# A hybrid encoder trunk on one NeuronCore: group A's softmax weights transposed as sixty-four-by-sixty-four quarters instead of whole 128 by 128 blocks

## The chip, the cores and the metric

The kernel runs on one NeuronCore of a Trainium2 chip. The metric is the device time of one execution in microseconds; the figure to compare is the median of several runs. The engines are named as in the profile: PE is TensorE's matmul, PEld its weight load, DVE VectorE, ACT ScalarE, POOL GpSimd, SP SyncE, which issues most DMAs.

## The reference

Two layers, each over 1024 tokens of 1024 channels. What matters here is group A, six heads of 64 channels whose attention runs over a mixture of three windows with dilations 1, 4 and 16:

```python
for (w, d) in DILATED_PAIRS:                      # (128,1), (512,4), (2048,16)
    half = w // (2 * d)
    ...
    o, l = banded_attention(to_sub(q), to_sub(k), to_sub(v), bias_table, half, half, d)
wts = jax.nn.softmax(jnp.stack(lses, 0), axis=0)
return jnp.einsum('gbsh,gbshd->bshd', wts, jnp.stack(outs, 0))
...
pexp = jnp.exp(logits - m[..., None])             # inside banded_attention
out = jnp.einsum('nbgrqk,nbkgd->nbqgrd', pexp, vb.astype(jnp.float32))
```

Beside group A a layer has windowed attention (group B), an mLSTM (group C), one input and one output projection, a SwiGLU feed-forward layer and a gated embedding.

## The kernel before, in words

Everything is float32. The large projections split each operand into a high and a low part and issue three matmuls per block of 128 rows (`product`, L219 to L221, 128x512 each); attention multiplies in plain float32.

`group_a` works on units `(p, g, i)`: three head pairs `p`, two groups of windows `g`, four steps `i`; 24 units in each layer, 48 in all. The heads of a pair are called `e` = 0, 1. A unit has three stages:

- `score` (L529 to L537): queries times keys for two tiles of 128 queries, each head into a PSUM bank of its own (`psc`). Bias and row maximum follow on DVE (L549), the exponential on ACT (L550); the result is `pr`, two tiles of 128 queries by 512 weights.
- `flip` (L555 to L570): each `pr` is turned so that keys stand on the partitions. Four 128 by 128 transposes on PE fill one bank (`ppt`, L563), one bank per head; DVE copies the first head's bank to SBUF (`pT`, L568), ACT the second's (L566).
- `weigh` (L572 to L597): `pT` times values into `po` (L584), copied to `u` on DVE (L587 to L592).

The steps are staggered: step `n` issues `score(n)`, `weigh(n-2)`, `flip(n-1)`. Between two steps PE works on the input projection. Which instruction of which stream comes next on PE is set by `mix`, which advances the streams by estimated costs (`yield` values); `flip` counts 1000 there, as before the change. The order inside DVE, ACT and POOL is chosen by the framework's scheduler when the program is built, from estimated durations, and is then fixed. PE has one queue for all streams: whatever stands behind a waiting matmul waits too.

While the first head pair is under way, a side stream computes the gates of group C (`gates`, L828 to L900): bias (L843, L844), exponentials on ACT (L845 to L849), then two pairs of scans on DVE (L858 `gb`, L859 `gm`), an exponential on ACT (L866 `q`) and short operations (L864 to L882). `combine_a` merges the windows; its matmuls with 64 columns of weights and 32 moving columns are L635. Group C's `weigh` has products with 64 columns of weights and 65 moving columns (L1007). The input projection's evacuations are L399 and L401 (`z`). PSUM has six rotating banks for all of these and two more for the projection.

Of the kernel before, what the change touches and what calls it, by code (L numbers as in the profile page):

```python
# [21 lines left out]
P = 128  # L22
# [60 lines left out]
class Trunk:  # L83
# [386 lines left out]
    def group_a(self, z):  # L470
# [3 lines left out]
        nc = self.nc  # L474
        units = [(p, g, i) for p in range(3) for g in range(2) for i in range(NCH // 2)]
        heads = (slice(0, 64), slice(64, 128))
# [78 lines left out]
        def flip(u):  # L555
            p, g, i = u
            pTs = []
            for e, pr in enumerate(st[u]):
                pt = self.bank("ppt")
                for b in range(4):  # L560

                    c = b if g == 0 else b % 2 * 2 + b // 2
                    nc.tensor.transpose(pt[:, c * P : c * P + P], pr[:, b * P : b * P + P], self.ident)  # L563
                pT = self.half("pT")
                if e:
                    nc.scalar.copy(pT, pt)  # L566
                else:
                    nc.vector.tensor_copy(pT, pt)  # L568
                pTs.append(pT)
            st[u] = pTs  # L570

# [26 lines left out]
        for i in range(n + 2):  # L598
            cost = 0.0
            if i < n:  # L600
                p = units[i][0]
                if units[i][1:] == (0, 0):
                    while ("k", p) not in z:
                        yield None
                    begin(p)
                    cost += 2000.0
                score(units[i])
                cost += 1000.0
                if units[i][1:] == (0, 3) and p < 2:
                    tables(p + 1)  # L610
            if 0 <= i - 2:
                weigh(units[i - 2])
                cost += 1000.0
            if 0 <= i - 1 < n:
                flip(units[i - 1])
                cost += 1000.0
            yield cost
# [1049 lines left out]
```

## Time and profile before

| what | value |
|---|---|
| median of 3 runs | 2799.74 us (2798.83 to 2800.63) |
| the profiled execution's own time | 2797.81 us |
| its span, first to last instruction | 2796.0 us |
| PE busy | 2670.7 us (96%), 13930 matmuls |
| DVE busy | 1920.4 us (69%) |
| ACT busy | 1129.1 us (40%) |
| mean granted TensorE clock | 0.978 of full speed |
| DMA, mean over the span | 92 GB/s |

The profiled execution took 1.8 us more than its span, and lies 1.9 us under the median. A row of the time line gives the start of an instruction or of a run of equal ones, how long it lasted, the engine, the line of the kernel, the operation, the tile written and those read, the shape and the count. For PE a shape such as 128*64 128x65 says how many rows and columns of the array were in use and what was streamed. Matmuls overlap, so what one of them costs is the distance between starts, not its duration. Of a matmul of plain float32 the trace shows more records than the program has instructions; counts in rows are of records.

### The profile page before, as it was taken

To read this page: it belongs to the slowest core of one execution; us is meant where nothing else is said; L and a number is where in the kernel's file an instruction comes from. 1 tells how busy PE (TensorE), PEld (TensorE's weight loads), DVE (VectorE), ACT (ScalarE), POOL (GpSimd) and SP (SyncE) were. 2 spreads that over 40 slices of the span, in tenths; PEclk is the share of its full clock that TensorE was granted. 3 is DMA by queue.
4 is the path that set the end of the run, shared out by engine and by line. 5 is a ranking of instruction groups with operands and counts; after the bars stand their busy time and mean duration, and the time that the engine had idled before them with its cause. 6 is when DMAs were issued, how large, how long until landed. Compare 5 with 4: busy or idle time off the path is not lost.

```text
span 2796.0 us, 37474 instructions
## 1 busy us (share of the span) xinstructions
PE 2670.7 (96%) x13930; PEld 2124.0 (76%) x13930; DVE 1920.4 (69%) x3019; ACT 1129.1 (40%) x2301; POOL 966.8 (35%) x724
## 2 busy tenths in 40 slices
PE   8999998998999999999999999989899999989997
PEld 6777776676888887788777778857678888877887
DVE  8654866579665558997655448564986565599957
ACT  5443253544333324344445433543443333333444
POOL 3112433136332325660121123431553333276302
PEclk9999999999999999999999999999899999999999
DMA  4010145132222235312321012542232222632124
GB/s 146 28 65 31 42 110 174 56 129 72 95 77 82 91 109 189 116 61 68 114 82 54 32 38 71 116 148 97 79 113 76 83 91 72 207 133 86 46 83 136
DMA packets 134618, 258.57 MB, mean 92 GB/s; under 512 B 14649, under 2 KB 55649, under 8 KB 134436
## 3 DMA queue, kind: packets, MB, share of 16 engines
q1 hardware_dynamic: 130740, 244.51, 26.7%
q0 software_dynamic: 3696, 11.66, 1.2%
q8 instruction: 110, 1.80, 0.3%
q14 instruction: 72, 0.59, 0.1%
HBM read 206.19 MB, written 49.93 MB: 92 GB/s over the span
## 4 chain that ended last, share of the span: by engine, by line
PE 77%; DVE 12%; issue 4%; POOL 2%; ACT 2%; DMA 2%; SPq 0%; DVEq 0%; POOLq 0%; ACTq 0%
PE pd L219 10%; PE pd L220 9%; PE pd L221 9%; PE pd L1270 9%; PE pd L1269 9%; PE pd L1271 9%; PE pd L1410 3%; PE pd L1411 3%; PE pd L1409 3%; PE po L584 1%; PE ppt L563 1%; DVE f L134 1%; DVE x L1234 1%; DVE x L1382 1%; DVE wr L1336 1%
## 5 line engine op out<-in xcount | busy, mean ns | idle before, releaser
L1270 PE MATMUL pd<-r,wf 128*128 128x512 f32 x1232 | 494.0, 401 | 16.4 <-POOL r L1229 9.3
L1269 PE MATMUL pd<-r,wf 128*128 128x512 f32 x1232 | 490.1, 398 | 11.3 <-ACT r L1228 11.3
L1271 PE MATMUL pd<-r,wf 128*128 128x512 f32 x1232 | 488.9, 397 | 0.0
L219 PE MATMUL pd<-h,wh 128*128 128x512 f32 x832 | 339.3, 408 | 12.7 <-ACT h L133 6.8
L220 PE MATMUL pd<-h,wh 128*128 128x512 f32 x832 | 329.4, 396 | 2.8 <-DVE h L134 1.7
L221 PE MATMUL pd<-h,wl 128*128 128x512 f32 x832 | 328.0, 394 | 1.0 <-DVE wl L134 1.0
L1288 DVE TENSOR_TENSOR g<-g,pd 128x512 f32<-128x512 f32 x264 | 176.8, 684 | 219.0 <-PE pd L1271 218.9
L1270 PEld LDWEIGHTS pd<-r,wf 128*128 128x128 f32 x1232 | 234.7, 191 | 81.7 <-POOL r L1229 19.2
L1269 PEld LDWEIGHTS pd<-r,wf 128*128 128x128 f32 x1232 | 235.1, 191 | 67.0 <-ACT r L1228 13.0
L1271 PEld LDWEIGHTS pd<-r,wf 128*128 128x128 f32 x1232 | 235.3, 191 | 52.3
L134 POOL TENSOR_TENSOR f<-wr,f 128x512 fp32r<-128x512 f32 x120 | 181.2, 1523 | 154.7 <-ACT f L133 127.9
L1410 PE MATMUL pd<-f,f 128*128 128x512 f32 x560 | 221.3, 395 | 12.9 <-DVE f L134 12.9
L1409 PE MATMUL pd<-f,f 128*128 128x512 f32 x560 | 220.3, 393 | 5.4 <-DVE x L1382 5.4
L1411 PE MATMUL pd<-f,f 128*128 128x512 f32 x560 | 220.8, 394 | 4.2 <-POOL f L134 4.1
L133 ACT CAST f<-wr 128x512 fp32r<-128x512 f32 x240 | 137.9, 619 | 192.6 <-PE pd L1410 90.7
L133 ACT CAST wf<-s 128x512 fp32r<-128x512 f32 x176 | 105.0, 619 | 272.4 <-POOL s L200 121.1
L134 DVE TENSOR_TENSOR wf<-s,wf 128x512 fp32r<-128x512 f32 x176 | 176.2, 1002 | 42.8 <-ACT wf L133 41.6
L134 POOL TENSOR_TENSOR wl<-wr,wh 128x1024 fp32r<-128x1024 f32 (+1 forms) x44 | 109.3, 2483 | 249.9 <-ACT wh L133 139.5
L219 PEld LDWEIGHTS pd<-h,wh 128*128 128x128 f32 x832 | 158.0, 190 | 48.1 <-ACT h L133 6.8
L220 PEld LDWEIGHTS pd<-h,wh 128*128 128x128 f32 x832 | 158.0, 190 | 35.2 <-DVE h L134 2.6
L221 PEld LDWEIGHTS pd<-h,wl 128*128 128x128 f32 x832 | 157.7, 189 | 35.5 <-DVE wl L134 1.9
L197 POOL TENSOR_TENSOR s<-wr,s 128x512 f32<-128x512 f32 x44 | 59.1, 1344 | 307.1 <-DVE wf L134 307.1
(315 smaller groups left out, 5484.2 us busy)
## 6 DMA issues: line engine op xcount, KB each, us to landing
wr<-w_up SPq DMA_DIRECT2D x88, 512.0 KB, 3.7
wr<-w_in SPq DMA_DIRECT2D x52, 512.0 KB, 3.6
gd<-g SPq DMA_DIRECT2D x88, 256.0 KB, 2.0
wr<-w_down SPq DMA_DIRECT2D x80, 256.0 KB, 4.2
wr<-gd SPq DMA_DIRECT2D x80, 256.0 KB, 5.3
wr<-ple_gate SPq DMA_DIRECT2D x40, 512.0 KB, 3.5
ee<-md SPq DMA_DIRECT2D x32, 384.0 KB, 7.5
x<-xd SPq DMA_DIRECT2D x24, 512.0 KB, 4.3
```

The costliest lines, as they stand in the source:

```text
L133: self.pin(nc.scalar.copy(hi[:, cs], src))
L134: self.pin((eng or nc.vector).tensor_tensor(lo[:, cs], src, hi.bitcast(F32)[:, cs], OP.subtract))
L219: nc.tensor.matmul(ps, hi[:, ks], rh, start=k == 0, stop=False)
L220: nc.tensor.matmul(ps, hi[:, ks], rl, start=False, stop=False)
L221: nc.tensor.matmul(ps, lo[:, ks], rh, start=False, stop=k == n - 1)
L1269: nc.tensor.matmul(ps, hi[:, ks], rh, start=k == 0, stop=False)
L1270: nc.tensor.matmul(ps, hi[:, ks], rl, start=False, stop=False)
L1271: nc.tensor.matmul(ps, lo[:, ks], rh, start=False, stop=k == KT // 2 - 1)
L1288: add = lambda out, a, b, op=OP.add: nc.vector.tensor_tensor(out, a, b, op)
L1409: nc.tensor.matmul(ps, lh[:, cs], rh, start=k == 0, stop=False)
L1410: nc.tensor.matmul(ps, lh[:, cs], rl, start=False, stop=False)
L1411: nc.tensor.matmul(ps, ll[:, cs], rh, start=False, stop=k == K2 - 1)
```

## The change

`flip` no longer uses the transpose operation. It multiplies each 64 by 64 quarter of `pr` by a 64 by 64 part of the identity, as a plain float32 matmul. A quarter's position in the array follows from its partitions: queries of the lower or upper half choose the rows, keys of the lower or upper half the columns. Queries of the two halves go into different banks; a bank then holds both heads, four blocks and 64 queries, and each head's `pT` is gathered from both banks by two copies of 4 by 64 columns.

```diff
+            pts = [self.bank("ppt").rearrange("p (e c q) -> p e c q", e=2, c=4) for _ in heads]
             for e, pr in enumerate(st[u]):
-                pt = self.bank("ppt")
                 for b in range(4):
                     c = b if g == 0 else b % 2 * 2 + b // 2
-                    nc.tensor.transpose(pt[:, c * P : c * P + P], pr[:, b * P : b * P + P], self.ident)
+                    for ks in heads:
+                        for pt, qs in zip(pts, heads):
+                            nc.tensor.matmul(pt[ks, e, c], pr[qs, b * P + ks.start : b * P + ks.stop], self.ident[qs, qs], start=True, stop=True)
+            for e in range(2):
                 pT = self.half("pT")
-                if e:
-                    nc.scalar.copy(pT, pt)
-                else:
-                    nc.vector.tensor_copy(pT, pt)
+                for pt, qs in zip(pts, heads):
+                    dst = pT.rearrange("p (c q) -> p c q", c=4)[:, :, qs]
+                    if e:
+                        nc.scalar.copy(dst, pt[:, e])
+                    else:
+                        nc.vector.tensor_copy(dst, pt[:, e])
                 pTs.append(pT)
```

The change adds six lines, so later lines stand six lower in its listing (L584 becomes L590).

On PE, one step of the first head pair. The names are those above; `pd` is the projection. Before:

```order
L584 MATMUL po_677<-pT_650,va_542 64x128
L563 MATMUL ppt_685<-ident,pr_628 128x128 x4
L563 MATMUL ppt_692<-ident,pr_629 128x128 x4
L219 MATMUL pd_609<-h_174,wh_601 128x512
L220 MATMUL pd_609<-h_175,wh_601 128x512
```

With the change (sixteen rows stand for each `pr`; the first of each and the last are shown):

```order
L590 MATMUL po_703<-pT_675,va_542 64x128
L566 MATMUL ppt_711<-ident,pr_628 64x64
L566 MATMUL ppt_712<-ident,pr_628 64x64
...
L566 MATMUL ppt_711<-ident,pr_629 64x64
L566 MATMUL ppt_712<-ident,pr_629 64x64
...
L219 MATMUL pd_609<-h_174,wh_601 128x512
L220 MATMUL pd_609<-h_175,wh_601 128x512
```

Eight transposes have become thirty-two quarter products that alternate between two banks; what stands before and behind them is the same.

On DVE in layer 0, at the second pair of gate scans, near 97 us of the trace of before. Before:

```order
L587 COPY u_578<-po_920 128x2x128
L568 COPY pT_931<-ppt_926 128x512
L399 SCALAR_TENSOR_TENSOR z_819<-pd_826,rs_381 128x512
L858 SCALAR_TENSOR_TENSOR gb_830<-q_833,fg_596 32x1024
L859 SCALAR_TENSOR_TENSOR gm_831<-fg_596,ig_595 32x1024
```

With the change:

```order
L593 COPY u_578<-po_1050 128x2x128
L864 SCALAR_TENSOR_TENSOR gb_934<-q_937,fg_596 32x1024
L865 SCALAR_TENSOR_TENSOR gm_935<-fg_596,ig_595 32x1024
L574 COPY pT_1090<-ppt_1056 128x4x64
L574 COPY pT_1090<-ppt_1057 128x4x64
L399 SCALAR_TENSOR_TENSOR z_923<-pd_930,rs_381 128x512
```

The two scans have moved ahead of the copies that `weigh` of the same unit waits for, and ahead of an evacuation of the projection.

On ACT in layer 1, at the same place of the program. Before, the copy of `pT` stood ahead of the exponential of `gm` (L866); with the change it stands behind it (L872):

```order
L872 ACTIVATE q_12920<-gm_12917 64x1024
L572 COPY pT_13075<-ppt_13038 128x4x64
L572 COPY pT_13075<-ppt_13039 128x4x64
L133 CAST wh_13182<-wr_12906 128x1024
L550 ACTIVATE pr_13100,stat_12560<-pr_13100,stat_12560 128x256
```

The exponential needs the scans' result, so in layer 1 both halves of `pT` now stand behind the scans; on DVE the order there is as in layer 0, and a pair of `pT` copies of the unit before has in addition moved behind L852, just ahead of the first pair of scans.

## Rows read from the trace of the kernel before

**Rows 1.** Page, busy time by engine: us, share of span, instructions.
```profile
PE 2670.7 (96%) x13930; PEld 2124.0 (76%) x13930; DVE 1920.4 (69%) x3019; ACT 1129.1 (40%) x2301; POOL 966.8 (35%) x724
```
**Rows 2.** Windows: stretch, us, busy us (count) PE PEld DVE ACT POOL, clock, DMA, GB/s.
```profile
63.00:253.00 190.00, 186.08 (x1198) 140.45 (x1196) 109.53 (x312) 91.61 (x263) 32.10 (x25) 0.99 0.14 45
1448.00:1636.00 188.00, 185.42 (x1212) 140.68 (x1210) 96.23 (x291) 93.81 (x267) 31.93 (x25) 1.00 0.13 40
```
**Rows 3.** Groups by line and shape, PE: busy us, mean ns, idle before and releaser.
```profile
L563 PE MATMUL ppt<-ident,pr 128*128 128x128 f32 x384 | 53.1, 280 | 0.5 <-ACT pr L550 0.3
L529 PE MATMUL psc<-z,z 64*128 64x256 f32 x192 | 27.4, 402 | 0.0
```
**Rows 4.** Time line of PE, layer 0, one weigh and flip: start us, us.
```profile
98.08 1.69 PE L584 MATMUL po<-pT,va 128*64 128x256 f32 x8
99.69 1.09 PE L563 MATMUL ppt<-ident,pr 128*128 128x128 f32 x8
100.54 0.48 PE L219 MATMUL pd<-h,wh 128*128 128x512 f32 x1
100.86 0.39 PE L220 MATMUL pd<-h,wh 128*128 128x512 f32 x1
```
**Rows 5.** Time line of PE, combine_a's products and the projection behind them.
```profile
146.07 1.13 PE L635 MATMUL pst<-mj,div 128*64 128x32 f32 x32
147.12 0.50 PE L219 MATMUL pd<-h,wh 128*128 128x512 f32 x1
147.46 0.40 PE L220 MATMUL pd<-h,wh 128*128 128x512 f32 x1
```
**Rows 6.** Time line of PE, group C's products and the projection behind them.
```profile
387.51 1.62 PE L1007 MATMUL pso<-vc,ee 128*64 128x65 f32 x48
389.06 0.50 PE L219 MATMUL pd<-h,wh 128*128 128x512 f32 x1
389.40 0.40 PE L220 MATMUL pd<-h,wh 128*128 128x512 f32 x1
```
**Rows 7.** Copies out of ppt (L568, L566 group A): duration ns min/median/max.
```profile
L568 DVE COPY pT<-ppt x48: 668/680/692, 65.3 to 1632.9; 128x512 f32<-128x512 f32 x48
L566 ACT COPY pT<-ppt x48: 560/564/588, 67.0 to 1633.3; 128x512 f32<-128x512 f32 x48
L734 DVE COPY pT<-ppt x32: 408/550/551, 492.3 to 1929.6; 128x384 f32<-128x384 f32 x24, 128x256 f32<-128x256 f32 x8
L732 ACT COPY pT<-ppt x32: 346/464/482, 493.0 to 1929.7; 128x384 f32<-128x384 f32 x24, 128x256 f32<-128x256 f32 x8
```
**Rows 8.** Time line of DVE, layer 0, at the second pair of scans.
```profile
97.35 0.67 DVE L568 COPY pT<-ppt 128x512 f32<-128x512 f32 x1
98.65 2.28 DVE L858 TENSOR_TENSOR_SCAN gb<-q,fg 32x1024 f32<-32x1024 f32 x1
100.86 2.26 DVE L859 TENSOR_TENSOR_SCAN gm<-fg,ig 32x1024 f32<-32x1024 f32 x1
```
**Rows 9.** Time line of PE, layer 0, the projection's next stop (in brackets idle, releaser).
```profile
109.27 0.39 PE L221 MATMUL pd<-h,wl 128*128 128x512 f32 x1
112.53 0.50 PE L219 MATMUL pd<-h,wh 128*128 128x512 f32 x1 [2.87 <-DVE z L399]
```
**Rows 10.** Windows, right behind that stop, columns as in rows 2.
```profile
113.50:117.00 3.50, 3.50 (x10) 2.69 (x10) 0.19 (x1) 1.05 (x1) 0.49 (x1) 0.52 0.44 150
```
**Rows 11.** Time line of DVE, layer 1, at the second pair of scans.
```profile
1482.13 0.67 DVE L568 COPY pT<-ppt 128x512 f32<-128x512 f32 x1
1482.83 2.28 DVE L858 TENSOR_TENSOR_SCAN gb<-q,fg 32x1024 f32<-32x1024 f32 x1
1485.04 2.25 DVE L859 TENSOR_TENSOR_SCAN gm<-fg,ig 32x1024 f32<-32x1024 f32 x1
```
**Rows 12.** Time line of ACT and of PE, layer 1, the same place.
```profile
1487.33 1.06 ACT L866 ACTIVATE q<-gm 64x1024 f32<-64x1024 f32 x1 [3.44 <-DVE gm L859]
1496.64 0.50 PE L219 MATMUL pd<-h,wh 128*128 128x512 f32 x1 [2.21 <-ACT z L401]
```

## The prediction

> **What bounds the kernel now.** I read the page's busy times first: PE is busy for 96% of the span [rows 1]. Then the windows of the two stretches in which group A's flips stand: of 378 us PE is busy 371.5, DVE 206, ACT 185, at a granted clock of 0.99 and 1.00, so at the 2.4 GHz level [rows 2]. There PE is the bound, the projection fills every gap, and a longer flip on PE lengthens the program. Next come the records of a float32 product: 96 score matmuls in the program (four in each of 24 units) left 192 records [rows 3], so a plain product is two records; the 384 transposes left 384 [rows 3], one each. The time lines of PE give the paces [rows 4 to 6], and the time lines of DVE and ACT the place where the new order matters [rows 8, 11, 12].
>
> **Term 1, the quarter products.** A flip now takes from its first transpose at 99.69 to the second projection matmul at 100.86, 1.17 us [rows 4]; I count to that second matmul because the first also pays for the change of shape. Eight transposes start in 0.85 us, 0.106 each [rows 4].
>
> The change issues 32 products, 64 records, per flip. No row shows quarters. The nearest are products with 64 columns of weights on half the array's columns: 32 records, which I read as 16 rounds of two side by side, take 1.39 us to the second projection matmul (146.07 to 147.46) [rows 5]; 48 records, 24 rounds, take 1.89 us [rows 6]. The difference, 8 rounds in 0.50 us, makes a round 0.0625 us, though one streams 32 columns and the other 65; so I take the 64 columns of weights to set the round. What is left of 1.39 us after 16 rounds, 0.39 us, is the hand-over to whole-array matmuls, which the transposes hardly pay: that part is new.
>
> If four quarters run side by side as two do, a flip is 16 rounds and 1.39 us: 0.22 us more than now, 48 x 0.22 = 10.6 us. This is the lower bound. If only two run at a time it is 32 rounds, 32 x 0.0625 + 0.39 = 2.39 us, 1.22 us more, 58.6 us in all: the upper bound. I take a value near the lower bound, because column halves already work side by side in rows 5 and 6, score's products use 64 rows each [rows 3], and the change gives the two row halves different banks, as score does. Two more quarters must be fed in a round; half of a transpose's pace is 0.053, so a pair's round has 0.0095 us on top of its weights, and I add half of that, 0.005 us a round, 0.08 us a flip. A flip then costs 1.47 us, 0.30 more: **48 x 0.30 = 14.4 us**.
>
> **Term 2, the copies.** Two copies of 256 columns take the place of one of 512. Copies of 256 columns are the shortest of group B's: 408 ns on DVE, 346 on ACT, against 680 and 564 for 512 [rows 7]. DVE gains 48 x (816 - 680) = 6.5 us of work, ACT 48 x (692 - 564) = 6.1 us. I cost them at nothing: DVE has 172 us and ACT 193 us free in these 378 us [rows 2], and `weigh` stands one step, some 5 us, behind its flip. Where that cover is gone, each costs about 0.13 us, except at the place of term 3.
>
> **Term 3, the new order on DVE and ACT.** In both layers the second pair of gate scans now stands ahead of the `pT` copies that a `weigh` waits for, and the whole projection is queued behind that `weigh` on PE. One pair of scans takes 4.5 us (98.65 to 103.12) [rows 8].
>
> Layer 0: four flips of the first pair lie ahead of the gates, so the chain starts 1.2 us later. Where the copy stood (97.35) the scans now begin at about 98.6 and end at 103.1; two copies of 0.41 us end at 103.9. PE, which would be there at 98.08 + 6 x 0.30 = 99.9, waits until then, some 4 us. About 1.0 us remain of weigh, the flip takes 1.15 us to the projection, which then has 8.95 us of work (100.54 to 109.5) [rows 4, 9]: it is through at 115.0. Today PE is through at 109.5 but waits for the copy of `z` until 112.53 [rows 9]. So PE is 2.5 us later, where seven flips alone make 2.1: 0.4 us more. Behind today's stop the clock fell to 0.52, the 1.2 GHz level: ten matmuls in 3.5 us instead of 2.3 [rows 10]; I let the earlier stop pay the same.
>
> Layer 1: the chain is late by 1.2 us, and by 0.8 us more for the copies that moved ahead of the first scans. Scans in place of the copy at 1482.13 [rows 11] begin at 1484.1 and end at 1488.6. ACT now runs the 1.06 us exponential first [rows 12], then its two copies: 1490.4. With 1.0, 1.15 and 8.95 us as above PE is through at 1501.5, against 1496.64, where it waits 2.21 us for ACT today [rows 12]. That is 4.9 us, and a stop of over 5 us should cost a fall of the clock as in rows 10, 1.2 us, which the 2.21 us stop did not: 6.1 us, 4.0 more than the seven flips.
>
> Together **4.4 us**; the bounds are 0 (a stop of today absorbs what moves) and about 9 (both waits unabsorbed).
>
> **Sum.** 14.4 + 4.4 = 18.8 us. On the profiled execution's 2797.81 us that is 2816.6; the median of the runs lies 1.9 us higher, so **2818.5 us**.
>
> **Rival 1: two quarters at a time.** The array may overlap row halves or column halves, but not both, when a product is two records that must follow each other. For it: only pairs appear in the trace. Against it: the halves are free of each other in rows and columns, and the banks are separate. It decides where a round of four costs two rounds: 58.6 + 4.4 = 63 us, 2863.
>
> **Rival 2: a fixed cost per record.** 32 and 65 moving columns ran at the same pace [rows 5, 6], which is also what a fixed cost of 0.031 us a record would show; then 64 records take 2.0 us however they share the array, and the time is again about 2862. Against it: a fixed cost must be the same for transposes, which start every 0.106 us with twice the weights, and twice the pace fits the weights as well. The Trainium skill, TensorEngine Tiling (Array Packing), section Instruction Overhead, states such a cost: about 60 cycles a matmul, whatever it streams below that. At 2.4 GHz that is, as an estimate from this page, 25 ns, 1.6 us for 64 records, 2.0 us a flip and about 2843; no run here shows 64 records of four tiles.
>
> **Rival 3, faster: one record a quarter.** If a product with an identity were issued like a transpose, as one record, a flip would be 8 rounds: 8 x 0.0675 + 0.39 = 0.93 us, 0.24 less than now, -11.5 us and with term 3 about 2793. It decides below 11.6 rounds a flip ((1.17 - 0.39) / 0.0675). For it: transposes are one record. Against it: every plain float32 product of the trace is two [rows 3], and the change calls the plain product. The same page, section Restrictions and Gotchas, has column tiling exclude the transpose mode for float32 inputs; by it this rival falls.
>
> **Rival 4: no change.** If four quarters overlap even better than pairs (0.055 us a round: 1.27 us a flip, +4.8 us) and the stops of today absorb term 3, the sum stays under 5.6 us.
>
> **How the numbers follow.** A measurement can tell about 0.2%, 5.6 us, from no change: 2794.1 to 2805.3. Forecast 0.61; rival 1 0.17; rival 2 0.09; rival 3 0.06; rival 4 0.07. The forecast's own range is 2807 (10.6 us, less about 3 us for flips that hide in the two stops) to 2828 (term 3 at 9, rounds of 0.07). Rivals 1 and 2 hold a quarter, so the range must reach them: 2806 to 2863 leaves out rivals 3 and 4 and a part of rival 1, under 2 in 10. Faster 0.06, same 0.07, slower 0.87.
>
> **What would show it.** In the profile of the changed kernel: L566 with 3072 records, and 64 of them with the hand-over in about 1.47 us on PE's time line (2.4 for rivals 1 and 2, 0.9 with 1536 records for rival 3); copies of about 410 and 350 ns, 96 each; PE waiting for `pT` near 100 us and 1486 us, for some 4 and 5 us, with the clock near 0.5 behind it; the stops on `z` near 112 and 1496 us gone. A flip under 1.3 us or no wait at those two places would make the prediction wrong.

## The result, and the profile after

The change made the kernel slower: 2817.48 us (median of 4 runs, 2815.43 to 2817.78) against 2799.70 us for the kernel before in the same comparison (4 runs, 2798.83 to 2800.63). The ratio is 1.0062, with a 95% interval of 1.0044 to 1.0079; that is +17.8 us. The profiled execution took 2817.52 us, with a span of 2815.7.

From the page of the changed kernel, the busy time by engine:

```profile
PE 2681.5 (95%) x16618; PEld 2133.4 (76%) x16618; DVE 1929.0 (69%) x3067; ACT 1136.2 (40%) x2349; POOL 966.0 (34%) x724
```

PE has 2688 records more than before [rows 1]: 3072 for the quarters less 384 for the transposes. DVE is 8.6 us and ACT 7.1 us busier, with 48 more copies each. The lines of the quarters and of the copies, as count, duration min/median/max in ns, first and last start, shapes:

```profile
L566 PE MATMUL ppt<-ident,pr x3072: 217/218/366, 64.3 to 1652.5; 64*64 64x64 f32 x192
L574 DVE COPY pT<-ppt x96: 406/415/426, 66.3 to 1653.1; 128x256 f32<-128x256 f32 x96
L572 ACT COPY pT<-ppt x96: 345/372/380, 67.6 to 1653.6; 128x256 f32<-128x256 f32 x96
```

The time line of PE around a flip in which nothing waits (start, duration, then the operation):

```profile
81.56 1.16 PE L566 MATMUL ppt<-ident,pr 64*64 64x64 f32 x64
82.65 0.50 PE L219 MATMUL pd<-h,wh 128*128 128x512 f32 x1
82.99 0.39 PE L220 MATMUL pd<-h,wh 128*128 128x512 f32 x1
```

From the first quarter to the second projection matmul this takes 1.43 us; with transposes it took 1.17 [rows 4]. The 0.26 us divide in two. The records' own starts run over 0.944 us, where eight transposes took 0.820: 0.124 us more. From the last record to the second projection matmul pass 0.148 + 0.337 us, where it was 0.028 + 0.318: 0.139 us more, the hand-over. Ahead of the flip nothing is new: from the last matmul of `weigh` to the first record it is 0.31 us in both traces.

The time line of PE at the second pair of gate scans, layer 0 and then, below the dots, layer 1 (in brackets the idle time before, and who ended it):

```profile
104.23 1.12 PE L590 MATMUL po<-pT,va 128*64 128x256 f32 x2 [4.60 <-DVE pT L574]
105.77 1.97 PE L590 MATMUL po<-pT,va 128*64 128x256 f32 x6 [0.42 <-ACT pT L572]
107.67 1.99 PE L566 MATMUL ppt<-ident,pr 64*64 64x64 f32 x64
109.58 0.71 PE L219 MATMUL pd<-h,wh 128*128 128x512 f32 x1
...
1499.48 2.94 PE L590 MATMUL po<-pT,va 128*64 128x256 f32 x8 [4.75 <-DVE pT L574]
1502.35 1.30 PE L566 MATMUL ppt<-ident,pr 64*64 64x64 f32 x64
1503.58 0.50 PE L219 MATMUL pd<-h,wh 128*128 128x512 f32 x1
```

Both waits for `pT` are there, and the stops on `z` of [rows 9, 12] are gone. The time line of DVE at the first of them shows why `weigh` waits: two scans of 2.2 us stand ahead of the copies.

```profile
98.93 2.28 DVE L864 TENSOR_TENSOR_SCAN gb<-q,fg 32x1024 f32<-32x1024 f32 x1
101.14 2.25 DVE L865 TENSOR_TENSOR_SCAN gm<-fg,ig 32x1024 f32<-32x1024 f32 x1
103.42 0.76 DVE L574 COPY pT<-ppt 128x256 f32<-128x256 f32 x2
```

The windows behind the two waits, columns as in rows 2:

```profile
104.20:107.50 3.30, 2.85 (x8) 1.05 (x8) 3.23 (x6) 2.42 (x4) 0.71 (x1) 0.50 0.00 0
107.50:110.50 3.00, 3.00 (x68) 2.63 (x68) 2.96 (x13) 2.08 (x8) 2.78 (x2) 0.57 0.52 175
...
1499.40:1502.30 2.90, 2.82 (x8) 1.04 (x8) 2.77 (x6) 1.91 (x4) 0.83 (x1) 0.50 0.00 0
1502.30:1505.00 2.70, 2.70 (x71) 2.37 (x71) 2.65 (x5) 0.00 (x0) 2.62 (x2) 0.93 0.58 193
```

After each wait `weigh` and the flip run at a granted clock of 0.50 and 0.57, the 1.2 GHz level, in layer 0, and at 0.50 and then 0.93 in layer 1.

One thing the forecast did not have is in the time line of ACT at the same place:

```profile
103.88 0.37 ACT L572 COPY pT<-ppt 128x256 f32<-128x256 f32 x1 [4.22 <-DVE pT L574]
104.27 1.05 ACT L872 ACTIVATE q<-gm 64x1024 f32<-64x1024 f32 x1
105.34 0.37 ACT L572 COPY pT<-ppt 128x256 f32<-128x256 f32 x1
```

Both heads now share each bank, and ACT's copy of the second head starts only when DVE has copied the first head out of the same bank; before, where it waited at all, it was for PE (4.6 us, 2 times). Its second half then stood behind an exponential of 1.05 us, which is the 0.42 us in the second row of PE above.

How far the same matmul of the rest of the program has moved against the trace of before, in us, worked out by counting the matmuls of each line, for the changed kernel and for six kernels that follow below:

```
time in before     125.4    255   1170   1190   1448   1505   1640   2785
changed kernel       4.5    8.3    6.8   10.5   10.5   15.8   19.6   19.5
e2                   1.4    5.2    4.8    6.9    6.9   12.2   16.0   18.3
e5                  -2.9   -5.5   -5.1   -1.5   -1.4    0.3   -3.1   -2.7
e6                  -4.9   -4.9   -5.2   -5.2   -5.2   -7.4   -7.4   -4.5
e7                  -2.8    0.9   -0.3    2.4    2.4    2.6    6.5    7.0
e9                  -6.9  -10.3   -9.7   -9.7   -9.7  -12.5  -15.9  -17.2
e11                 -4.8   -5.2   -4.8   -2.9   -2.9   -5.3   -5.7   -3.4
```

In the changed kernel group A of layer 0 (to 255 us) gives 8.3 us and that of layer 1 (1448 to 1640) 9.1. The other 2.1 us come in the down projection of layer 0: 1.5 us are lost again by 1170, and 3.7 are gained between 1170 and 1190 us. There PE stands twice for an operand `f` of that projection. Its time line in the kernel before, in the changed kernel, and in e1, the changed kernel run again:

```profile
1181.18 0.50 PE L1410 MATMUL pd<-f,f 128*128 128x512 f32 x1 [0.57 <-DVE f L134]
1184.57 0.50 PE L1410 MATMUL pd<-f,f 128*128 128x512 f32 x1 [0.36 <-DVE f L134]
...
1185.59 0.50 PE L1416 MATMUL pd<-f,f 128*128 128x512 f32 x1 [0.90 <-DVE f L134]
1190.65 0.50 PE L1416 MATMUL pd<-f,f 128*128 128x512 f32 x1 [2.05 <-DVE f L134]
...
1185.32 0.50 PE L1416 MATMUL pd<-f,f 128*128 128x512 f32 x1 [0.90 <-DVE f L134]
1190.38 0.66 PE L1416 MATMUL pd<-f,f 128*128 128x512 f32 x1 [2.05 <-DVE f L134]
```

From 1190 to 1200 us the granted clock is 0.83 in the changed kernel, and 1.00 in the kernel before. The longer stop is not the chance of one execution, since e1 has it to the hundredth; e5 and e10 have it too. It does not come with the quarters either: e8, with the same flips, has 0.57 and 0.38 us, and e6 and e9 are as before. DVE, ACT and POOL have the same order there in both kernels. What decides between the two lengths was not tried, and stays open.

### The profile page after: what moved, and what is told of

It reads as the page before. It is cut to its first block, busy times and chain, and to the rows that moved or that the text cites. A ratio compares the mean times of both kernels' runs of the same rounds, so it can differ in the third digit from the quotient of the medians.

```text
span 2815.7 us, 42948 instructions
## 1 busy us (share of the span) xinstructions
PE 2681.5 (95%) x16618; PEld 2133.4 (76%) x16618; DVE 1929.0 (69%) x3067; ACT 1136.2 (40%) x2349; POOL 966.0 (34%) x724
## 4 chain that ended last, share of the span: by engine, by line
PE 78%; DVE 12%; issue 4%; DMA 2%; POOL 2%; ACT 2%; SPq 0%; DVEq 0%; POOLq 0%; ACTq 0%
PE pd L219 10%; PE pd L220 10%; PE pd L221 10%; PE pd L1276 9%; PE pd L1275 9%; PE pd L1277 9%; PE pd L1416 3%; PE pd L1417 3%; PE pd L1415 3%; PE ppt L566 2%; PE po L590 2%; DVE x L1240 1%; DVE f L134 1%; PE psc L713 1%; DVE x L1388 1%
## 5 line engine op out<-in xcount | busy, mean ns | idle before, releaser
L1276 PE MATMUL pd<-r,wf 128*128 128x512 f32 x1232 | 492.7, 400 | 17.8 <-POOL r L1235 9.6
L1275 PEld LDWEIGHTS pd<-r,wf 128*128 128x128 f32 x1232 | 234.8, 191 | 68.2 <-ACT r L1234 14.4
```

The costliest lines, as they stand in the source:

```text
L1275: nc.tensor.matmul(ps, hi[:, ks], rh, start=k == 0, stop=False)
L1276: nc.tensor.matmul(ps, hi[:, ks], rl, start=False, stop=False)
```

## Experiments

They ran in three groups, on three chips, with the kernel before beside each. Its medians were 2802.98 us (e1 to e4; 9 runs, 2799.41 to 2806.30), 2801.46 (e5 to e8) and 2800.37 (e9 to e11): the differences below go by these.

### The changed kernel again, and its old order on DVE

e1 has no edit. e2 keeps the quarters and holds the two scans behind what was traced before them:

```diff
-            nc.vector.tensor_tensor_scan(v(b), v(q1), v(lf), 0.0, OP.mult, OP.add)
-            nc.vector.tensor_tensor_scan(v(m), v(lf), v(ig), 0.0, OP.add, OP.max)
+            self.tc.keep_in_program_order(nc.vector.tensor_tensor_scan(v(b), v(q1), v(lf), 0.0, OP.mult, OP.add))
+            self.tc.keep_in_program_order(nc.vector.tensor_tensor_scan(v(m), v(lf), v(ig), 0.0, OP.add, OP.max))
```

> The changed kernel again, beside the next runs. Theory (flips dearer by 0.263 us each, 46 to 48 of them 12.1 to 12.6 us, plus some 5 us for weigh waiting behind the second gate scans in both layers): 2817.5 us, +17.8 us. Rival (the chip of the first comparison, or the 2.5 us that its trace gained between 1094 and 1183 us, where the change does nothing, made part of the difference): +15 us or less.

> The change, but the gate scans may not be moved ahead of what is traced before them, so that the two pT copies stand in front of the second pair of scans on DVE again, in both layers. Theory: the waits of weigh for pT near 104 and 1499 us (4.60 and 4.75 us) go, the stops on z near 112 and 1496 us come back, and only the flips' own price is left: 48 x 0.263 = 12.6 us over the kernel before, 2812.3 us, some 5 us less than the change. Rival 1 (the order costs nothing, the stops on z ate it): within 1.5 us of the change, 2816 to 2819. Rival 2 (the scans are now late for the state's chain and cost elsewhere): 2817 or more.

Measured: e1 2820.62 us, ratio 1.0059 (1.0046 to 1.0071), +17.6 us: the difference comes again in a second comparison. e2 2818.06 us, ratio 1.0057 (1.0043 to 1.0070): 2.6 us under e1, with intervals that overlap. My 5 us did not come, though the waits for `pT` did go. The offsets say where they stayed. In layer 0 the old order is 3.1 us better at 125 us, of which 0.9 us stood between the two traces before the first flip; in layer 1 nothing is gained (from 1448 to 1505 us 5.3 us in both). The time line of PE in e2 shows the stops on `z` back, and longer than before:

```profile
113.95 0.50 PE L219 MATMUL pd<-h,wh 128*128 128x512 f32 x1 [3.45 <-DVE z L399]
...
1507.24 0.50 PE L219 MATMUL pd<-h,wh 128*128 128x512 f32 x1 [3.62 <-ACT z L401]
1507.58 0.54 PE L220 MATMUL pd<-h,wh 128*128 128x512 f32 x1
1507.92 0.63 PE L221 MATMUL pd<-h,wl 128*128 128x512 f32 x1
```

The second was 2.21 us [rows 12]. The time line of ACT in e2 gives the reason: the copy of `z` stands behind two exponentials of the gates, of which the first waits for DVE.

```profile
1504.44 1.06 ACT L887 ACTIVATE q<-q 64x1024 f32<-64x1024 f32 x1 [0.91 <-DVE q L884]
1505.53 1.05 ACT L888 ACTIVATE q<-gu 64x1024 f32<-64x1024 f32 x1
1506.60 0.58 ACT L401 COPY z<-pd 128x512 f32<-128x512 f32 x1
```

Behind it the clock fell (0.59 in the 2.8 us from 1507.2); behind the stop of before it had stayed at 1.00. So my theory fell in its second half: the order is not "scans ahead or not", but which of several waits in the gate block PE meets, and putting one right made another longer.

### The gate block without stops, with and without quarters

e6 is the kernel before; e7 is the change with e2's edit. In both the operations of `gates` behind the scans (seven of DVE, three exponentials of ACT) are held in the order in which they are traced:

```diff
-        nc.vector.tensor_tensor(nM[:R], b[:R], m[:R], OP.subtract)
+        self.tc.keep_in_program_order(nc.vector.tensor_tensor(nM[:R], b[:R], m[:R], OP.subtract))
...
-        nc.scalar.activation(q1[:R], q1[:R], AF.Exp)
-        nc.scalar.activation(q1[64:128], u[:R], AF.Exp)
+        self.tc.keep_in_program_order(nc.scalar.activation(q1[:R], q1[:R], AF.Exp))
+        self.tc.keep_in_program_order(nc.scalar.activation(q1[64:128], u[:R], AF.Exp))
```

> The kernel before with nothing of the change, but the gates' operations behind the scans (the copies, sums and exponentials on DVE and ACT) are held in the order in which they are traced, so that the copies of z out of the projection's banks stand in front of them. Theory (what the change's order touched is a stop on z that the kernel before has too): the stop of 3.26 us near 112 us and the fall of the clock behind it (about 1.2 us) and the stop of 2.6 us near 1496 us go: 5 to 7 us faster than the kernel before, 2793 to 2795 us if that one takes 2799.7. Rival (the gates' chain, now later, is waited for elsewhere): within 1.5 us, or slower.

> The change with both orders held: the pT copies in front of the second pair of scans, and the copies of z in front of the gates' later operations. No stop of over 1 us should be left on PE in group A, so that the flips' own price stands alone. Theory: 48 x 0.263 = 12.6 us over the kernel of the run before this one (e6), and 5 to 7 us under the one with the old order alone (e2). Rival (the flips' price is partly hidden or doubled by DVE and ACT, whose copies cost 6 us more each): 9 us or less, or 16 or more, over e6.

Measured: e6 2793.51 us, ratio 0.9973 (0.9962 to 0.9983), 8 us faster than the kernel before, without any change to the flips. e7 2809.15 us, ratio 1.0031 (1.0018 to 1.0043), 7 to 9 us under e2 (as differences from the kernel before, and as medians). In e6's time line of DVE the copy of `z` now stands in front of the gates' chain, and the window where [rows 9] had the stop is full, at full clock:

```profile
106.85 0.68 DVE L399 SCALAR_TENSOR_TENSOR z<-pd,rs 128x512 f32<-128x512 f32 x1
107.45 1.21 DVE L870 TENSOR_TENSOR gm<-gb,gm 64x1024 f32<-64x1024 f32 x1
108.69 2.25 DVE L873 COPY gex<-gm 32x8 f32<-32x8 f32 x1
```
```profile
109.50:112.50 3.00, 3.00 (x15) 2.49 (x14) 2.95 (x5) 0.21 (x1) 2.50 (x3) 1.00 0.19 42
112.50:117.00 4.50, 4.50 (x21) 3.72 (x21) 2.45 (x5) 3.24 (x5) 1.85 (x1) 1.00 0.58 148
```

The offsets give 4.9 us for this in layer 0 (the stop of 3.26 us between starts and the slow matmuls behind it) and 2.2 in layer 1.

e7 against e6 is the flips with their copies, and little else. By the offsets: 0.9 + 4.9 = 5.8 us to 255 us, and from 1448 to 1640 us 4.1 + 2.2 = 6.3 us, 12.1 in all, where 48 x 0.263 is 12.6; 0.9 of the 12.1 us stood between the two traces before the first flip. By the medians it is 15.6 us, with intervals of some 3 us on each side; that sits between my theory and the rival's 16, and the medians alone don't decide. The traces do: group A has no second price of that size.

### Plain products in whole tiles, and quarters by pairs

e3 keeps the whole blocks and makes plain products of them; e4 keeps the quarters and issues all of the lower half of the queries first. Both with e2's edit.

```diff
-                    nc.tensor.transpose(pt[:, c * P : c * P + P], pr[:, b * P : b * P + P], self.ident)
+                    nc.tensor.matmul(pt[:, c * P : c * P + P], pr[:, b * P : b * P + P], self.ident, start=True, stop=True)
```
```diff
-            for e, pr in enumerate(st[u]):
-                for b in range(4):
+            for pt, qs in zip(pts, heads):
+                for e, b in [(e, b) for e in range(2) for b in range(4)]:
+                    pr = st[u][e]
...
-                        for pt, qs in zip(pts, heads):
```

> The tiles of before (whole 128 by 128, one copy of 512 columns), but each transpose written as a plain float32 product with the identity; scans held in the old order. Tells the price of two records a product from the price of the small tiles. Theory: 16 records a flip, each at a transpose's pace of 0.106 to 0.117 us, so 0.85 to 0.94 us more a flip, 48 flips 41 to 45 us: 2841 to 2845 us, and no gap before the first projection matmul (28 ns as with transposes). Rival 1: a transpose is two passes in one record, and plain records start twice as often: 2797 to 2803 us. Rival 2: the gap before the projection comes with plain products and not with small tiles: 48 x 0.139 = 6.7 us more than either, with the gap of 148 ns in the trace.

> The change with the scans in the old order, but each flip issues all 16 quarters of the lower half of the queries (rows 0 to 63) before those of the upper half, so that neighbours in the queue share two tiles and not four. Theory (records start in the order of the queue, four tiles at work only if four stand side by side in it): 32 rounds of 0.059 us in place of 16, 0.94 us more a flip, 45 us: about 2857 us. Rival 1 (the array takes later records past waiting ones): as the kernel with the old order, about 2812 us. Rival 2 (a row half's two tiles follow each other faster than 0.059 us when nothing else runs): in between, 2820 to 2850.

Measured: e3 2838.48 us, ratio 1.0126 (1.0110 to 1.0142), +35.5 us, just under the theory's 2841 to 2845; e4 2843.64 us, ratio 1.0144 (1.0130 to 1.0158), +40.7 us, under the theory's 2857 and in the range of its second rival. Both flips stand in the time lines of PE, e3's and then e4's:

```profile
82.26 2.05 PE L563 MATMUL ppt<-ident,pr 128*128 128x128 f32 x16
84.06 0.48 PE L219 MATMUL pd<-h,wh 128*128 128x512 f32 x1
84.38 0.40 PE L220 MATMUL pd<-h,wh 128*128 128x512 f32 x1
```
```profile
83.97 1.91 PE L565 MATMUL ppt<-ident,pr 64*64 64x64 f32 x64
85.81 0.50 PE L219 MATMUL pd<-h,wh 128*128 128x512 f32 x1
86.15 0.39 PE L220 MATMUL pd<-h,wh 128*128 128x512 f32 x1
```

In e3 sixteen records leave every 0.118 us, and the flip takes 2.12 us. The last of them is followed by the projection within 0.03 us, as after transposes: the hand-over belongs to the small tiles, not to plain products. In e4 the same 64 records as in the change need 1.69 us instead of 0.94, since neighbours share two tiles: 2.18 us a flip. So records start in the order of the queue, and the change's order, which names four different tiles in a row, is worth 0.75 us a flip. It is also what the forecast's first rival would have looked like. A round of two takes 0.054 us here, less than the 0.059 of e4's theory, as its second rival had it.

The flips' differences in the traces, 48 x 0.95 = 46 us and 48 x 1.01 = 48 us, are some 8 to 10 us more than the medians show. Trace against trace it is as the flips say: the profiled runs of e3 and e4 (2844.11 and 2844.85 us) lie 46.3 and 47.0 us above that of the kernel before (2797.81). The medians are set against a kernel before that took some 5 us longer in this group; and the runs of e3 spread from 2832.6 to 2844.1 us, with the profiled one the slowest.

### Row halves: as transposes, and as plain products

e5 issues two transposes per block, one for each half of the rows, into the change's two banks. e10 does the same with plain products. Both with e2's edit.

```diff
-                    for ks in heads:
-                        for pt, qs in zip(pts, heads):
-                            nc.tensor.matmul(pt[ks, e, c], pr[qs, b * P + ks.start : b * P + ks.stop], self.ident[qs, qs], start=True, stop=True)
+                    for pt, qs in zip(pts, heads):
+                        nc.tensor.transpose(pt[:, e, c], pr[qs, b * P : b * P + P], self.ident[qs, qs])
```

> Each whole transpose becomes two transposes of one record each, one for the rows of either half of the queries (64 rows by 128 columns of weights, 64 columns streamed), into the two banks of the change, two copies of 256 columns as there, scans in the old order. Tells whether the weights' columns or the streamed columns set a round. Theory (0.92 ns per column of weights: 0.059 us for 64, 0.118 for 128 in the plain products of the whole array): 8 rounds of two at about 0.11 us, 0.82 us from first to last pair as with whole transposes, plus the 0.139 us of the gap to the projection that small tiles showed: 48 x 0.14 to 0.25 = 7 to 12 us over the kernel before. Rival (the streamed columns count, 64 in place of 128): 8 rounds of 0.055 to 0.06 us, a flip 0.36 - 0.14 = 0.2 to 0.25 us shorter, 10 to 12 us faster than the kernel before.

> The row halves of e5 as plain float32 products with the identity: 64 rows by 128 columns of weights, 64 columns streamed, two records each, 32 records a flip; scans in the old order. Tells what sets a plain product's round. Theory of the prediction (the columns of weights set it, 0.059 us for 64): 16 rounds of 0.118 us, 1.8 us from first to last record, and with the gap to the projection 1.1 us a flip over whole transposes, 48 x 1.1 = 53 us over the kernel before. Rival (the streamed columns set it, as e5 showed for transposes): 16 rounds of 0.06 to 0.07 us, 0.9 to 1.1 us from first to last, 0.25 to 0.4 us a flip, 12 to 19 us over the kernel before, about the price of the change.

Measured: e5 2792.35 us, ratio 0.9972 (0.9961 to 0.9983), 8 to 9 us faster than the kernel before, against my theory and near its rival's 10 to 12; e10 2847.86 us, ratio 1.0166 (1.0152 to 1.0180), +47.5 us, for my theory. The time lines of PE, e5's and then e10's:

```profile
78.65 0.71 PE L565 MATMUL ppt<-ident,pr 64*128 64x64 f32 x16
79.29 0.50 PE L219 MATMUL pd<-h,wh 128*128 128x512 f32 x1
79.63 0.40 PE L220 MATMUL pd<-h,wh 128*128 128x512 f32 x1
```
```profile
83.39 2.00 PE L565 MATMUL ppt<-ident,pr 64*128 64x64 f32 x32
85.32 0.50 PE L219 MATMUL pd<-h,wh 128*128 128x512 f32 x1
85.65 0.39 PE L220 MATMUL pd<-h,wh 128*128 128x512 f32 x1
```

Same tiles, same 64 streamed columns, same weights. As transposes eight pairs start within 0.49 us, 0.07 us a pair, and the flip takes 0.98 us, 0.19 less than with whole transposes although it pays the hand-over too. As plain products sixteen pairs take 1.73 us, 0.115 us a pair, the pace of 128 columns of weights in e3. So a plain product goes by the columns of its weights, as the forecast took it, and a transpose does not. That holds for the 32 to 128 streamed columns of these rows: the products of `weigh`, with 64 columns of weights but 256 streamed, start every 0.101 us in the trace of before, against 0.029 us for those of [rows 5].

### The copies

e8 is e2 with the copies shared out by bank; e11 is the kernel before with only its copies split in two.

```diff
-                for pt, qs in zip(pts, heads):
+                for h, (pt, qs) in enumerate(zip(pts, heads)):
...
-                    if e:
+                    if h:
```
```diff
-                if e:
-                    nc.scalar.copy(pT, pt)
-                else:
-                    nc.vector.tensor_copy(pT, pt)
+                for qs in heads:
+                    dst, src = (t.rearrange("p (c q) -> p c q", c=4)[:, :, qs] for t in (pT, pt))
+                    if e:
+                        nc.scalar.copy(dst, src)
+                    else:
+                        nc.vector.tensor_copy(dst, src)
```

> The change with the scans in the old order, but the two copies of a bank are made by one engine (the first bank by DVE for both heads, the second by ACT), where the change lets ACT's copy of a bank stand behind DVE's. Theory (that wait is covered, since weigh stands a step of some 5 us behind its flip): within 1.5 us of e2, the kernel with the old order, and in the trace the copies on ACT wait for PE instead of DVE. Rival (weigh waits for ACT's second copy): 48 x up to 0.35 us, 3 to 15 us faster than e2.

> The kernel before with its whole transposes, and only the copies split as in the change: two of 256 columns (four pieces of 64) in place of one of 512, on the same engine; the order on DVE as before. Theory (covered work): within 1.5 us of the kernel before. Rival (each flip's longer copies are waited for): 48 x 0.13 = 6 us slower, or more.

Measured: e8 2817.52 us, ratio 1.0059 (1.0047 to 1.0072), +16.1 us, where e2 has +15.1: no gain, so ACT's wait for DVE is covered, at least with the scans in their old order. In e8 the copies on ACT list PE as what they waited for (5.1 us, 2 times), where the change lists DVE (10.2 us, 4 times).

e11 2793.94 us, ratio 0.9980 (0.9970 to 0.9989), 6 us faster, which neither theory had. By the offsets it is level with the kernel before (within 0.1 us) up to 109 us, through seven flips with longer copies, and then gains 4.8 us at once, and 2.4 in layer 1 near 1496. Its time line of DVE says what happened:

```profile
107.05 1.21 DVE L872 TENSOR_TENSOR gm<-gb,gm 64x1024 f32<-64x1024 f32 x1
108.18 0.68 DVE L399 SCALAR_TENSOR_TENSOR z<-pd,rs 128x512 f32<-128x512 f32 x1
108.78 1.76 DVE L875 COPY gex<-gm 32x8 f32<-32x8 f32 x1
```

The framework's scheduler, with other durations for the copies, put the copy of `z` ahead of the longest operation of the gates' chain (`gex`) by itself, one place behind where e6 has it by hand; in the kernel before it stood three operations later. The copies cost nothing; the order that came with them was worth 6 us.

### The two gains together

e9 is e5's row halves with the orders of e7, no other edit.

> The row-half transposes of e5 together with the orders of e7 (pT copies in front of the second scans, z copies in front of the gates' later operations). Theory (the two gains come from different waits and add): e5 was 8 us and e6 8 us under the kernel before, so 13 to 16 us under it, about 2787 us where that one takes 2801. Rival (the stops on z were already paying for part of the shorter flips): 8 to 10 us under it.

Measured: e9 2785.41 us, ratio 0.9947 (0.9935 to 0.9960), 15 us under the kernel before and some 32 under the change, each taken against the kernel before of its own group. They add nearly in full, and this version beats both kernels. In the table, from 1448 to 1640 us, e6 gains 2.2 us and e9 6.2, so the row halves 4.0, where 24 x 0.19 is 4.6. PE's time line has no start-to-start gap of over 0.9 us left in either stretch of group A behind its first step.

## Why the prediction was right, and where its parts were off

The forecast was 2818.5 us, the result 2817.5. The two prices it is added up from were there, each with the cause that it gave; that the sum came within 1 us is partly luck. By the offsets group A moved the program by 17.4 us, 0.6 of which stood before the first flip: 16.8 us against a forecast of 18.8. The other 2.1 us came in the down projection, where the forecast had nothing.

**Term 1, the quarter products.** A flip of 1.43 us against a forecast of 1.47; 48 x 0.263 = 12.6 us against 14.4. Not all of it arrived: by the offsets the 17 flips of a layer behind the second pair of scans moved the program by 3.8 us and not by 4.5. Four quarters do run side by side: 64 records in 0.944 us are 16 rounds of about 0.06 us. The 0.005 us a round that I added for feeding four tiles is not there; the rounds cost the 0.0625 of [rows 5, 6] or a little less. It had also come from a misread pace: 0.85 us runs to the projection's start, and eight transposes start in 0.820 us, seven steps of 0.117 and not 0.106. What is left of a flip behind 16 rounds of 0.060 is 0.47 us, where I had 0.39; and transposes pay most of that too, 0.35 us, so only 0.139 is new. That weights set the round of a plain product held, by e3 and e10: 0.118 and 0.115 us for 128 columns, with 128 and with 64 streamed.

**Term 2, the copies at nothing.** Right as far as was tried: the medians are 415 and 372 ns against the 408 and 346 of [rows 7], and e11 and e8 show them covered. What the term left out is that ACT's copies now queue behind DVE's, and that new durations let the scheduler re-sort the program; both had to be seen in the order, not in the copies' time.

**Term 3, the new order.** The waits came where it put them, 4.60 and 4.75 us for "some 4" and "over 5", with the clock down behind both and the stops on `z` gone. Its price: in layer 0 the first seven flips and their waits moved the program by 3.9 us (4.5 less the 0.6 that it was late before the first flip), less 7 x 0.263 = 1.8 for the flips, so 2.0 us where I had 0.4. In layer 1 it is 15.8 - 10.5 = 5.3, less 1.8, so 3.5 where I had 4.0. Together 5.5 against 4.4. The layer-0 error is the step "About 1.0 us remain of weigh, the flip takes 1.15 us to the projection": at a clock of 0.50 and 0.57, and with the half-bank copy behind an exponential, weigh and flip took from 104.23 to 109.58, 5.4 us, in place of 2.2. I let the earlier stop "pay the same" in clock; it paid more, since `weigh` and a flip of small tiles fell into the slow stretch.

What I did not see is that the term's opposite, the kernel before's own order, was no clean baseline: e6 takes 8 us out of it with the flips untouched. The order is worth about two thirds of the flips' price, and e2 shows that undoing one half of it gains 2.6 us, with intervals that overlap.

**The rivals.** Two quarters at a time: refuted by 0.944 us a flip, and e4 is what it would cost, 2843.6 us with the scans in the old order. That is less than the 2863 I gave it, in part because a round of two takes 0.054 us and not 0.0625. A fixed cost per record: refuted; records start every 15 ns in the change, 27 ns in e4, 33 ns in e5. The Trainium skill, TensorEngine Tiling (Array Packing), section Instruction Overhead, gives some 60 cycles a matmul; with four tiles at work this trace shows 36 cycles' worth of time per record (15 ns at 2.4 GHz), and each record has a weight load of its own, so the measurement decides against it as a cost of every record in the queue. Counted by the program's products, two records each, it is 30 ns or 72 cycles, and that the trace does not contradict. One record a quarter: refuted, 3072 records. Its idea was sound for row halves: e5 splits the array with one record each, and is faster. No change: refuted, +17.8 and +17.6 us. The upper end of the forecast's own range was added up wrongly: rounds of 0.07 us and 9 us for term 3 make 2825, not 2828.

The same page of the Trainium skill, section Tiling Modes, Key Properties, says that a change of tiling mode drains the engine. The trace agrees with it and gives a size: 0.139 us more from the last small-tile record to the second projection matmul. e3, with plain products in whole tiles, does not have it.

## What to carry to other kernels

In this kernel transposing float32 through plain products costs two records each and the time of the weights' columns. Keep the transpose operation; if the array is to be split, split it by rows, where it still is one record and two halves run side by side (0.98 us a flip against 1.17 whole and 1.43 in quarters). Four tiles only work together if four different ones stand side by side in the queue. When a scheduler orders the engines, a new duration can re-sort them: price the order as a term of its own, look for copies out of PSUM that stand behind a long chain on their engine, and hold those few by hand; here that was worth 8 us, as much as the split by rows.

## What the runs showed that was not expected

- Float32 transposes of 64 rows: a pair every 0.07 us, with 128 columns of weights, where plain products of the same shape need 0.115 us a pair (e5, e10). The streamed columns fit it (64 here, 128 in a whole transpose, 0.117 us); I have no run that varies them alone.
- A round of four quarters costs 0.060 us, a round of two 0.054 (e4): the third and fourth tile add a ninth to the round.
- Splitting each flip's two copies, with no other edit, made the kernel 6 us faster (e11), through the order of a stage that the edit does not touch.
- Two stops of 3.45 and 3.62 us between projection matmuls were followed by a granted clock of 0.69 and 0.59 over the next 3 us (e2); behind the stop of 2.21 us in the kernel before [rows 12] it stayed at 1.00.
